# A two-layer encoder in split float32: the neighbourhood bias is loaded with its mask folded in, three weight tiles get their low parts by accumulating transfers, a fourth moves to VectorE, and one mean is issued later

## The chip, the cores and the metric

The program runs on one core of one Trainium2 chip. The metric is the device time of one execution in microseconds; before the change the median of three runs is 1551.98 us (1550.17 to 1553.2). Besides the times there is one execution taken with the hardware profiler. Its engines are called PE (TensorE), DVE (VectorE), ACT (ScalarE), POOL (GpSimd) and SP (SyncE, which here only issues transfers).

## What is computed

Two layers of an encoder on 512 positions of width 1024, all in float32. The parts that the change touches:

```python
mem_n = rms_norm(mem, mem_norm_g)                     # 256 memory tokens
for l in range(DEPTH):                                # 2
    h = rms_norm(x, g_pre_mix[l])
    proj = h @ w_in[l]                                # 1024 -> 5632: q,k,v of A and B, q of M, gates
    o_a = neighborhood_attention(...)                 # 6 heads, s = q.k*scale + bias, softmax, @ v
    o_b = dilated_attention(...)
    o_m = memory_attention(q_m, mem_n, w_mem_kv[l])   # kv = mem_n @ w_mem_kv[l]
    merged = sum of sigmoid gates * (o_x @ w_br_x)
    x = x + rms_norm(merged @ w_out[l], g_post_mix[l])
    h = rms_norm(x, g_pre_ffn[l])
    u = depthwise_conv_centred(h @ w_up[l], conv_w[l], conv_b[l])
    a, b = split(u)
    x = x + rms_norm((gelu(a) * b) @ w_down[l], g_post_ffn[l])
```

In neighbourhood attention each query sees a window of 8 rows by 16 columns of the 8 x 64 grid. The kernel computes 256 candidate keys for each block of 128 queries and adds to the scores a bias by relative position; keys outside the window get -1e30.

## The kernel before, in words

**Split matmuls.** Every float32 operand of a large matmul is held as two tiles in the PE's rounded float32 format (float32r): a high part, which is the rounded value, and a low part, which is the rest. `mm3` (line 249) issues three matmuls for one product: high x high, high x low of the activations, low of the weights x high. So the low part of a weight tile is first read by the third matmul of a trio.

**Weights.** `weights` (line 227) loads a tile of 128 x 1024 numbers (512 KB) on SP's queue into one of three `wraw` buffers, then `split` (line 223) makes the parts: ACT copies `wraw` into the high tile and, by default, DVE subtracts (`tensor_sub`) to make the low tile. With `eng` the subtraction goes to POOL. Tiles that are loaded ahead of their use are split in two halves of 512 columns, each with its own pair of buffers `m` (pool of 32) or `h`.

**Order of the work.** The order on PE is written by the program: `Woven` keeps a modelled PE clock, and jobs (Python generators) are resumed when the clock has reached their due time; `yield 3.5` means "go on 3.5 us of modelled PE time later". PE's instructions are chained in that order. A job that asks for a mean too early makes PE wait for the sums. The order on the other engines comes out of a scheduler that works from the same program; each engine takes its instructions strictly in order.

**The stretch between the layers.** The last product of layer 0 (`sublayer_end`, line 815, with the weights `w_down`) is finished for columns 0 to 255 first, then for 256 to 511. For the first half `end_job` (line 379) takes a mean of squares (a matmul with a column of 1/1024, tile `mean`), spreads it over the partitions by a transpose (matmul with `ident`), multiplies the eight output tiles `y` by it and adds them to `x` on DVE, squares `x` on ACT and adds the squares up on DVE (`acc`). Then `pre_norm_job` (line 364) asks for the next mean from that `acc`. Meanwhile PE works on the memory projection of layer 1 (`mem_kv`, line 479, four tiles of `w_kv`, here called kv0 to kv3) and then, in `run_group` (line 501), on six tiles of `w_in` (g0 to g5). These ten tiles are fetched ahead by `kv_ahead` (line 1013) and line 1029. Which engine makes a tile's low part is read from two strings in line 38: `KVE` for kv0 to kv3 and `GEN` for g0 to g5 (V for DVE, G for POOL). In `KVE` the first letter is unused, since kv0 always takes DVE. For the second half `raw_end_job` (line 418) does the same with tiles `ka` that are not normed yet, and asks for its last mean `yield 3.5` after its squares (line 436).

**The bias.** `a_bias` (line 593) runs one head ahead of `a_head_job`. On POOL's queue it fetches 128 x 256 numbers for a head, and POOL then makes three tiles `mask - bias` (128 x 256, line 599), for the left edge, the middle and the right edge of the grid. The constant `mask` (384 KB) comes in at the start. k is scaled by -0.125, so that PE's scores are negated; DVE adds the negated bias and takes the minimum in one instruction (line 617).

Of the kernel before, what the change touches and what calls it, by code (L numbers as in the profile page):

```python
# [7 lines left out]
F32 = mybir.dt.float32  # L8
# [7 lines left out]
GRID_W = 64  # L16
# [21 lines left out]
SQG, LOG, GEN, KVE = {0: (), 1: ()}, {0: (), 1: ()}, 'GGVGVG', 'VVGG'  # L38
# [81 lines left out]
def tile_hybrid_encoder(ctx, tc, xT, memT, memg, vecs, rpb, w_in, w_kv, w_bra, w_brb, w_brm,  # L120
                        w_out, w_up, w_down, c_ident, c_mask, c_tab0, c_tab1, out):
# [58 lines left out]
    DUP, MDUP = G, G  # L180
    MSQ = G
# [31 lines left out]
    mask = const.tile([128, 3, 256], F32, name="mask")  # L213
# [204 lines left out]
    def raw_end_job(l, goff, og, acc, acc2, nxt, lat):  # L418
# [17 lines left out]
        yield 3.5  # L436
# [156 lines left out]
    def a_bias(l, h):  # L593
        n01, n2r = ytile((128, 2, 256)), ytile((128, 2, 256))
        raw = n2r[:, 1, :]
        behind(nc.gpsimd.dma_start(out=raw, in_=rpb[l, h]).ins, last_lo.get(G))
        neg = (n01[:, 0, :], n01[:, 1, :], n01[:, 1, :], n2r[:, 0, :])
        for c, n in ((0, neg[0]), (1, neg[1]), (2, neg[3])):
            nc.gpsimd.tensor_sub(n, mask[:, c, :], raw)
        return neg  # L600

    def a_head_job(l, h, qkv, neg, oa):
# [293 lines left out]
    for t, c in ((mask, c_mask), (tab0, c_tab0), (tab1, c_tab1)):  # L896
        nc.sync.dma_start(out=t, in_=c)
# [4 lines left out]
    for l in range(depth):  # L902
# [99 lines left out]
        else:  # L1002
# [10 lines left out]
            def kv_ahead(l=l, pre=pre, gw=gw):  # L1013
                pre.append(weights(w_kv[l + 1, 0], KD, 128, htile))
                yield KVD
                for i in (1, 2, 3):
                    yield 0.9
                    pre.append(weights(w_kv[l + 1, i], KD, 128, big, G if KVE[i] == 'G' else V))
                wv.give(f"kv{l + 1}")
                for m in range(NG):  # L1020
                    yield GWD
                    gw.extend(group_weights([w_in[l + 1, FIRST[m]]], [G if GEN[m] == 'G' else V]))
# [6 lines left out]
            gw += group_weights([w_in[l + 1, m] for m in FIRST[NG:]], [G if e == 'G' else V for e in GEN[NG:]])  # L1029
# [4 lines left out]
def _consts():  # L1034
# [4 lines left out]

    mask = np.empty((3, 128, 256), f32)  # L1040
    for n, b in enumerate((0, 1, 3)):
        c = 16 * b + np.arange(16)
        kc = 16 * b - 8 + np.arange(32)
        start = np.clip(c - 8, 0, GRID_W - 16)[:, None]
        ok = (kc[None, :] >= start) & (kc[None, :] < start + 16)
        ok = np.broadcast_to(ok.reshape(1, 16, 2, 1, 16), (8, 16, 2, 8, 16)).reshape(128, 256)
        mask[n] = np.where(ok, 0.0, BIG)
    mask = np.ascontiguousarray(mask.transpose(1, 0, 2))
# [5 lines left out]
    for s in range(2):  # L1054
# [5 lines left out]
    return {"c_ident": ident, "c_mask": mask,  # L1060
            "c_tab0": tab0, "c_tab1": tab1.reshape(128, 2, 256)}


def _layout(inputs):
# [9 lines left out]
    def cols(v):  # L1074
# [13 lines left out]
    a["rpb"] = np.ascontiguousarray(pad[:, :, r - i + 7, 16 * t + c - 8 - cc + 31].reshape(L, NA_HEADS, 128, 256))  # L1088
# [13 lines left out]
        "c_ident", "c_mask", "c_tab0", "c_tab1"]  # L1102
# [22 lines left out]
```

## Time and profile before

| what | us |
|---|---|
| median of 3 runs | 1551.98 |
| the profiled execution, device time | 1551.73 |
| its span, first to last instruction | 1550.0 |
| PE busy | 1522.5 (98%) |
| DVE busy | 951.6 (61%) |
| ACT busy | 712.7 (46%) |
| POOL busy | 149.7 (10%) |

The span begins with the first instruction and ends with the last; all positions below are microseconds in it. "Idle before" of an instruction is the time for which its engine had nothing running, with the engine or transfer that let it go on. The granted clock is the share of TensorE's full speed that the throttle let through. Layer 0 lies up to about 800 us, layer 1 behind.

### The profile page before, as it was taken

The numbers are of one execution on the slowest core, as the hardware profiler recorded it, in microseconds if no ns is written. First come the engines' busy times: TensorE is split into PE (matmuls) and PEld (weight loads), VectorE is DVE, ScalarE is ACT, GpSimd is POOL, SyncE is SP. The second block draws the span as 40 slices with busy tenths as digits, with TensorE's granted clock in tenths as the row PEclk, the third lists the DMA queues.
The fourth block names the chain that finished last, engine by engine and source line by source line (L and its number), as shares of the span: only waits on it lengthen the run. The fifth ranks groups of instructions, "written<-read, shape, count | busy, mean of one in ns | idle before, by whom it ended". The sixth has DMA issues, their size and how long they took to land.

```text
span 1550.0 us, 20648 instructions
## 1 busy us (share of the span) xinstructions
PE 1522.5 (98%) x7970; PEld 1300.1 (84%) x7970; DVE 951.6 (61%) x1684; ACT 712.7 (46%) x1266; POOL 149.7 (10%) x217
## 2 busy tenths in 40 slices
PE   8999999999999999999989999999999999999997
PEld 7988888888988888888888888888889888888887
DVE  6685676335777777742497756753456977776233
ACT  5565554336544444532355555532354544444231
POOL 3340000110000000000154300002100000000000
PEclk9999999999999999999999999999999999999999
DMA  7221213235113322333431221132350233323331
GB/s 246 89 88 64 62 57 107 84 95 165 53 59 100 100 96 95 118 90 101 129 102 59 78 66 58 61 104 88 102 177 15 82 96 99 101 99 89 99 105 63
DMA packets 45810, 144.91 MB, mean 93 GB/s; under 512 B 5376, under 2 KB 9600, under 8 KB 45712
## 3 DMA queue, kind: packets, MB, share of 16 engines
q1 hardware_dynamic: 43776, 139.85, 28.5%
q10 hardware_dynamic: 1296, 2.10, 0.4%
q0 software_dynamic: 640, 1.64, 0.3%
q8 instruction: 62, 1.02, 0.3%
q14 instruction: 36, 0.29, 0.1%
HBM read 141.48 MB, written 2.10 MB: 93 GB/s over the span
## 4 chain that ended last, share of the span: by engine, by line
PE 91%; DVE 6%; ACT 2%; issue 1%; DMA 0%; SPq 0%; ACTq 0%; DVEq 0%
PE mm L247 80%; PE s L247 4%; PE o L247 3%; PE pt L258 2%; DVE m L114 1%; DVE y L114 1%; PE pt L247 1%; DVE ka L114 1%; DVE x L114 1%; ACT y L114 1%; DVE st L114 0%; DVE acc L114 0%; DMA x<-in_xT_dram 0%; DVE wlo L114 0%; ACT whi L114 0%
## 5 line engine op out<-in xcount | busy, mean ns | idle before, releaser
L247 PE MATMUL mm<-h,whi 128*128 128x512 f32 x2496 | 776.5, 392 | 0.0
L247 PEld LDWEIGHTS mm<-h,whi 128*128 128x128 f32 x2496 | 462.0, 188 | 91.3
L247 PE MATMUL mm<-h,wlo 128*128 128x512 f32 x1248 | 486.9, 390 | 0.0
L114 DVE TENSOR_TENSOR wlo<-wraw,whi 128x1024 fp32r<-128x1024 f32 (+1 forms) x213 | 259.2, 1217 | 284.7 <-ACT whi L114 282.3
L114 ACT CAST whi<-wraw 128x1024 fp32r<-128x1024 f32 (+1 forms) x213 | 221.4, 1040 | 307.8 <-PE mm L247 293.4
L247 PEld LDWEIGHTS mm<-h,wlo 128*128 128x128 f32 x1248 | 234.5, 188 | 49.6
L247 PE MATMUL mm<-m,whi 128*128 128x512 f32 (+1 forms) x800 | 215.1, 356 | 1.0 <-DVE m L114 0.8
L247 PEld LDWEIGHTS mm<-m,whi 128*128 128x128 f32 x800 | 141.8, 189 | 22.8 <-PE mm L247 1.3
L247 PE MATMUL mm<-m,wlo 128*128 128x512 f32 (+1 forms) x400 | 142.1, 355 | 0.0
L114 DVE SCALAR_TENSOR_TENSOR y<-y,vec,y 128x511 f32<-128x511 f32 x176 | 130.5, 748 | 3.5 <-ACT y L114 0.9
L114 DVE TENSOR_TENSOR y<-mm,R 128x512 f32<-128x512 f32 x82 | 56.4, 688 | 68.5 <-PE mm L247 68.5
L247 PEld LDWEIGHTS mm<-m,wlo 128*128 128x128 f32 x400 | 75.5, 189 | 10.9
L802 POOL TENSOR_TENSOR m<-m,y 128x512 f32<-128x512 f32 x28 | 36.1, 1289 | 399.4 <-DVE y L114 399.4
L114 ACT ACTIVATE y<-y,vec 128x512 f32<-128x512 f32 x88 | 71.1, 815 | 2.3 <-DVE y L114 1.9
L247 PE MATMUL mm<-m,m 128*128 128x512 f32 x240 | 63.5, 394 | 0.0
L114 ACT ACTIVATE y<-y 128x512 f32<-128x512 f32 x44 | 27.9, 633 | 71.7 <-DVE y L114 71.3
L114 ACT CAST m<-pt 128x512 fp32r<-128x512 f32 (+1 forms) x72 | 38.6, 541 | 46.8 <-PE pt L258 38.5
L114 ACT ACTIVATE y<-y,st 128x256 f32<-128x256 f32 (+1 forms) x80 | 43.8, 549 | 30.4 <-DVE st L114 28.9
L114 DVE TENSOR_TENSOR acc<-acc,sq 128x256 f32<-128x256 f32 (+1 forms) x80 | 41.1, 514 | 26.6 <-ACT sq L114 24.7
L114 DVE TENSOR_TENSOR m<-pt,m 128x512 fp32r<-128x512 f32 (+1 forms) x72 | 45.1, 630 | 19.9 <-ACT m L114 18.6
L114 ACT CAST m<-y 128x512 fp32r<-128x512 f32 x32 | 19.9, 622 | 72.5 <-DVE y L114 72.5
L247 PE MATMUL mm<-h,m 128*128 128x256 f32 x312 | 49.1, 301 | 2.0 <-ACT h L114 1.0
(154 smaller groups left out, 1789.9 us busy)
## 6 DMA issues: line engine op xcount, KB each, us to landing
wraw<-in_w_in_dram SPq DMA_DIRECT2D x88, 512.0 KB, 3.7
wraw<-in_w_up_dram SPq DMA_DIRECT2D x88, 512.0 KB, 3.6
wraw<-in_w_down_dram SPq DMA_DIRECT2D x32, 512.0 KB, 3.5
wraw<-in_w_out_dram SPq DMA_DIRECT2D x16, 512.0 KB, 3.9
wraw<-in_w_down_dram SPq DMA_DIRECT2D x16, 384.0 KB, 3.1
wraw<-in_w_kv_dram SPq DMA_DIRECT2D x8, 512.0 KB, 4.0
wraw<-in_w_bra_dram SPq DMA_DIRECT2D x16, 192.0 KB, 2.3
x<-in_xT_dram SPq DMA_DIRECT2D x8, 256.0 KB, 7.3
```

Source lines behind the costliest of these rows:

```text
L114: return op(*args, **kw)
L247: wv.pe(nc.tensor.matmul(ps, a, b, start=first, stop=last), cost)
L258: wv.pe(nc.tensor.transpose(ps[:, 128 * i:128 * i + 128], s, ident), 0.11)
L802: (V if br == 2 and m >= 6 else G).tensor_add(acc[m], acc[m], gs)
```

## The change

1. The host lays out the bias with the mask in it, three tables for each head instead of one; `a_bias` fetches them with two transfers on POOL's queue (256 and 128 KB) and computes nothing. `mask`, its load and the 36 subtractions on POOL are gone. k is scaled by +0.125, and line 617's instruction adds the bias and scales by -1.
2. In the strings, kv2, kv3 and g0 become `D`, and g1 becomes `V`. For `D`, ACT writes the high part and then, with a second instruction, minus the rounded value into the low tile; a transfer on POOL's queue then reads the weights from HBM again and adds them to the low tile (`accum_op=ALU.add`), for each half tile of 256 KB.
3. `raw_end_job` waits 5.0 instead of 3.5 us of modelled time before its last mean.

```diff
-SQG, LOG, GEN, KVE = {0: (), 1: ()}, {0: (), 1: ()}, 'GGVGVG', 'VVGG'
+SQG, LOG, GEN, KVE = {0: (), 1: ()}, {0: (), 1: ()}, 'DVVGVG', 'VVDD'
...
+    ENG = {'G': G, 'V': V, 'D': 'D'}
...
-    mask = const.tile([128, 3, 256], F32, name="mask")
...
             hi, lo = slot(F32R, (128, c, C)), slot(F32R, (128, c, C))
-            split(raw[:, k:k + c, :], hi, lo, eng)
+            if eng == "D":
+                last_copy[0] = ACT.copy(hi, raw[:, k:k + c, :]).ins
+                ACT.activation(lo, raw[:, k:k + c, :], AF.Copy, scale=-1.0)
+                nc.gpsimd.dma_start(out=lo, in_=src[:, k:k + c, :], accum_op=ALU.add)
+            else:
+                split(raw[:, k:k + c, :], hi, lo, eng)
...
         for k in range(KD):
             sumsq_add(acc2[:, half], xh(k, half), k == 0)
-        yield 3.5
+        yield 5.0
...
-        twice_split(ps, inner[:2], inner[2:], -0.125, DUP)
+        twice_split(ps, inner[:2], inner[2:], 0.125, DUP)
...
     def a_bias(l, h):
-        n01, n2r = ytile((128, 2, 256)), ytile((128, 2, 256))
-        raw = n2r[:, 1, :]
-        behind(nc.gpsimd.dma_start(out=raw, in_=rpb[l, h]).ins, last_lo.get(G))
-        neg = (n01[:, 0, :], n01[:, 1, :], n01[:, 1, :], n2r[:, 0, :])
-        for c, n in ((0, neg[0]), (1, neg[1]), (2, neg[3])):
-            nc.gpsimd.tensor_sub(n, mask[:, c, :], raw)
-        return neg
+        n01, n2r = ytile((128, 2, 256)), ytile((128, 256))
+        nc.gpsimd.dma_start(out=n01, in_=rpb[l, h, :, 0:2, :])
+        nc.gpsimd.dma_start(out=n2r, in_=rpb[l, h, :, 2, :])
+        return n01[:, 0, :], n01[:, 1, :], n01[:, 1, :], n2r
...
-                V.tensor_tensor_reduce(out=S[:, b2, :], in0=s[:, b2, :], in1=neg[b],
-                                               op0=ALU.add, op1=ALU.min, accum_out=m, scale=1.0, scalar=3e38)
+                V.tensor_tensor_reduce(out=S[:, b2, :], in0=s[:, b2, :], in1=pos[b],
+                                               op0=ALU.add, op1=ALU.min, accum_out=m, scale=-1.0, scalar=3e38)
...
-    for t, c in ((mask, c_mask), (tab0, c_tab0), (tab1, c_tab1)):
+    for t, c in ((tab0, c_tab0), (tab1, c_tab1)):
         nc.sync.dma_start(out=t, in_=c)
...
+    a["rpb"] = np.ascontiguousarray(np.where(np.stack(ok, 1), tab, tab.dtype.type(-BIG)))
```

What the change moves is shown by the order of the instructions on two engines. First POOL between the layers, before the change: behind the squares of the memory norm (`h<-h,sq`) stand the low parts (`m`) of kv2, kv3, g0 and g1, two each, and then the copies for `mem_kv`.

```order
L321 TENSOR_TENSOR h_1221_6214<-h_1221_6214,sq_1228_6234 128x256
L225 TENSOR_TENSOR m_6923<-wraw_6920,m_6922 128x512
L225 TENSOR_TENSOR m_6927<-wraw_6920,m_6926 128x512
L225 TENSOR_TENSOR m_6982<-wraw_6979,m_6981 128x512
L225 TENSOR_TENSOR m_6986<-wraw_6979,m_6985 128x512
L225 TENSOR_TENSOR m_7004<-wraw_7001,m_7003 128x512
L225 TENSOR_TENSOR m_7008<-wraw_7001,m_7007 128x512
```

The same place after the change.

```order
L326 TENSOR_TENSOR h_1221_6200<-h_1221_6200,sq_1228_6220 128x256
L245 DMA m_6909<-in_w_kv_dram 128x512
L245 DMA m_6914<-in_w_kv_dram 128x512
L245 DMA m_6970<-in_w_kv_dram 128x512
L245 DMA m_6975<-in_w_kv_dram 128x512
L245 DMA m_6994<-in_w_in_dram 128x512
L245 DMA m_6999<-in_w_in_dram 128x512
L298 COPY m_7063<-m_7063 64x256
```

The subtractions of kv2, kv3 and g0 have become six transfers in the same order, and the two of g1 (before, next behind the rows shown) are gone from POOL.

ACT at the same place, after the change: `m<-wraw` with CAST is a high part, with ACTIVATE the negated one that a transfer adds to; `st` is the root of the mean of the first half, `acc` and `sq` are its squares of `x`.

```order
L114 CAST m_6908<-wraw_6906 128x512
L114 ACTIVATE st_6897<-pt_6894,eps 128x2
L114 ACTIVATE m_6909<-wraw_6906 128x512
L114 CAST m_6913<-wraw_6906 128x512
L114 ACTIVATE m_6914<-wraw_6906 128x512
L114 CAST m_6969<-wraw_6967 128x512
L114 ACTIVATE m_6970<-wraw_6967 128x512
L114 ACTIVATE acc_6067<-x 128x256
L114 ACTIVATE sq_1337_6928<-x 128x256
L114 CAST m_6974<-wraw_6967 128x512
```

Before the change three high parts stood between the root and `acc`; now these are two high parts and three negated ones, and three more negated ones stand further on among the squares.

Next PE at the last mean of `raw_end_job`, before the change: `mm<-ka,m` are products of the raw second half with g0 and g1, three matmuls for each weight tile and each of eight `ka` tiles.

```order
L247 MATMUL mm_7273<-ka_7298,m_7026 128x256
L247 MATMUL pt_7516<-mean,acc_6081 128x1 x2
L247 MATMUL mm_7272<-ka_7299,m_7003 128x256 x2
L247 MATMUL mm_7272<-ka_7299,m_7004 128x256
L247 MATMUL mm_7273<-ka_7299,m_7025 128x256 x2
L247 MATMUL mm_7273<-ka_7299,m_7026 128x256
L247 MATMUL mm_7272<-ka_7300,m_7007 128x256 x2
L247 MATMUL mm_7272<-ka_7300,m_7008 128x256
L247 MATMUL mm_7273<-ka_7300,m_7029 128x256 x2
L247 MATMUL mm_7273<-ka_7300,m_7030 128x256
L247 MATMUL pt_7516<-ident,st_7519 128x128 x2
```

And after the change, from the third `ka` tile on.

```order
L252 MATMUL mm_7265<-ka_7290,m_7018 128x256
L252 MATMUL mm_7264<-ka_7291,m_6993 128x256 x2
L252 MATMUL mm_7264<-ka_7291,m_6994 128x256
L252 MATMUL mm_7265<-ka_7291,m_7017 128x256 x2
L252 MATMUL mm_7265<-ka_7291,m_7018 128x256
L252 MATMUL mm_7264<-ka_7292,m_6998 128x256 x2
L252 MATMUL mm_7264<-ka_7292,m_6999 128x256
L252 MATMUL mm_7265<-ka_7292,m_7021 128x256 x2
L252 MATMUL mm_7265<-ka_7292,m_7022 128x256
L252 MATMUL pt_7520<-mean,acc_6067 128x1 x2
```

The mean stands 12 matmuls later, and its transposes follow, as before, 12 matmuls behind it; nothing else on PE has another place.

More of the change, by code (lines that the diff above doesn't have):

```diff
@@ L120, in tile_hybrid_encoder @@
 def tile_hybrid_encoder(ctx, tc, xT, memT, memg, vecs, rpb, w_in, w_kv, w_bra, w_brb, w_brm,
-                        w_out, w_up, w_down, c_ident, c_mask, c_tab0, c_tab1, out):
+                        w_out, w_up, w_down, c_ident, c_tab0, c_tab1, out):
     nc = tc.nc
@@ L593, in a_bias, with a_head_job @@
     def a_bias(l, h):
-        n01, n2r = ytile((128, 2, 256)), ytile((128, 2, 256))
-        raw = n2r[:, 1, :]
-        behind(nc.gpsimd.dma_start(out=raw, in_=rpb[l, h]).ins, last_lo.get(G))
-        neg = (n01[:, 0, :], n01[:, 1, :], n01[:, 1, :], n2r[:, 0, :])
-        for c, n in ((0, neg[0]), (1, neg[1]), (2, neg[3])):
-            nc.gpsimd.tensor_sub(n, mask[:, c, :], raw)
-        return neg
-    def a_head_job(l, h, qkv, neg, oa):
+        n01, n2r = ytile((128, 2, 256)), ytile((128, 256))
+        nc.gpsimd.dma_start(out=n01, in_=rpb[l, h, :, 0:2, :])
+        nc.gpsimd.dma_start(out=n2r, in_=rpb[l, h, :, 2, :])
+        return n01[:, 0, :], n01[:, 1, :], n01[:, 1, :], n2r
+    def a_head_job(l, h, qkv, pos, oa):
         qs, ks, vs = qkv
@@ L767, in attention_job @@
     def attention_job(l, qkva, qkvb, qm, km, vm, oa, ob, om):
-        neg = a_bias(l, 0)
+        pos = a_bias(l, 0)
         for h in range(NA_HEADS):
@@ L771, in attention_job @@
             nxt = a_bias(l, h + 1) if h + 1 < NA_HEADS else None
-            wv.spawn(a_head_job(l, h, qkva, neg, oa))
-            neg = nxt
+            wv.spawn(a_head_job(l, h, qkva, pos, oa))
+            pos = nxt
             yield STEP_A
@@ L1017, in kv_ahead @@
                     yield 0.9
-                    pre.append(weights(w_kv[l + 1, i], KD, 128, big, G if KVE[i] == 'G' else V))
+                    pre.append(weights(w_kv[l + 1, i], KD, 128, big, ENG[KVE[i]]))
                 wv.give(f"kv{l + 1}")
@@ L1021, in kv_ahead @@
                     yield GWD
-                    gw.extend(group_weights([w_in[l + 1, FIRST[m]]], [G if GEN[m] == 'G' else V]))
+                    gw.extend(group_weights([w_in[l + 1, FIRST[m]]], [ENG[GEN[m]]]))
                 wv.give(f"gw{l + 1}")
@@ L1028, in tile_hybrid_encoder @@
             wv.need(f"gw{l + 1}")
-            gw += group_weights([w_in[l + 1, m] for m in FIRST[NG:]], [G if e == 'G' else V for e in GEN[NG:]])
+            gw += group_weights([w_in[l + 1, m] for m in FIRST[NG:]], [ENG[e] for e in GEN[NG:]])
             wv.need(f"h{l + 1}.{V_PRE}.0")
@@ L1038, in _consts @@
     ident = np.eye(128, dtype=f32)
[L1040 to L1048, printed above, removed]
     slopes = (f32(2.0) ** (-f32(8.0) * np.arange(1, 7, dtype=f32) / f32(6.0))).astype(f32)
@@ L1059, in _consts @@
         tab1[:, s, 1] = np.where(dj % 4 == 0, slopes[4 + s] * d, BIG)
-    return {"c_ident": ident, "c_mask": mask,
-            "c_tab0": tab0, "c_tab1": tab1.reshape(128, 2, 256)}
+    return {"c_ident": ident, "c_tab0": tab0, "c_tab1": tab1.reshape(128, 2, 256)}
 def _layout(inputs):
@@ L1087, in _layout @@
     i, cc, t, r, c = np.ogrid[:8, :16, :2, :8, :16]
-    a["rpb"] = np.ascontiguousarray(pad[:, :, r - i + 7, 16 * t + c - 8 - cc + 31].reshape(L, NA_HEADS, 128, 256))
+    tab = pad[:, :, r - i + 7, 16 * t + c - 8 - cc + 31].reshape(L, NA_HEADS, 128, 1, 256)
+    ok = []
+    for b in (0, 1, 3):
+        q = 16 * b + np.arange(16)
+        key = 16 * b - 8 + np.arange(32)
+        start = np.clip(q - 8, 0, GRID_W - 16)[:, None]
+        inside = (key[None, :] >= start) & (key[None, :] < start + 16)
+        ok.append(np.broadcast_to(inside.reshape(1, 16, 2, 1, 16), (8, 16, 2, 8, 16)).reshape(128, 256))
+    a["rpb"] = np.ascontiguousarray(np.where(np.stack(ok, 1), tab, tab.dtype.type(-BIG)))
     a["w_in"] = tiles(g["w_in"], 128)
@@ L1101 @@
 _INS = ["xT", "memT", "memg", "vecs", "rpb", "w_in", "w_kv", "w_bra", "w_brb", "w_brm", "w_out", "w_up", "w_down",
-        "c_ident", "c_mask", "c_tab0", "c_tab1"]
+        "c_ident", "c_tab0", "c_tab1"]
 def kernel(**inputs):
```

## The prediction

> **What bounds the kernel now.** PE is busy for 98% of the span, so time can only come from what PE does or from the few places where it stands. PE's instructions are the same before and after, but for one pair that moves; so the question is which of PE's waits go and which come. The list of PE's waits comes first (total, times, longest):
>
> ```profile
> PE pt L247 <- DVE acc L114: 4.6, 2, 3.5
> PE pt L247 <- DVE y L114: 3.2, 4, 2.0
> PE pt L258 <- DVE y L114: 2.1, 1, 2.1
> ```
>
> The first line is two waits for sums of squares (`acc`), both between the layers; the third is one wait in a head of layer 1. The second lies in the start, where the sums of the input are made. PE's timeline places the first:
>
> ```profile
> 777.09 3.04 PE L247 MATMUL mm<-h,m 128*128 128x256 f32 x24
> 783.59 0.58 PE L247 MATMUL pt<-mean,acc 128*128 128x1 f32 x4 [3.46 <-DVE acc L114]
> 784.03 1.62 PE L247 MATMUL mm<-h,m 128*128 128x256 f32 x9
> 785.76 0.69 PE L342 MATMUL pt<-ident,st 128*128 128x128 f32 x2
> 786.10 4.79 PE L247 MATMUL mm<-h,m 128*128 128x256 f32 x30
> ```
>
> PE ends kv1 at 780.13 and stands 3.46 us for the mean of `pre_norm_job`. Behind the wait it is slow as well: 24 matmuls took 3.04 us before it (0.127 each), 30 took 4.79 after it (0.160). The stretches with the granted clock (the figure ahead of the last two) say why:
>
> ```profile
> 785.00:787.00 2.00, 1.90 (x10) 1.61 (x9) 1.57 (x6) 0.64 (x3) 1.87 (x6) 0.50 0.04 8
> 787.00:789.00 2.00, 2.00 (x14) 2.00 (x14) 1.85 (x6) 0.80 (x2) 0.26 (x1) 0.69 0.00 0
> 812.00:815.00 3.00, 1.84 (x17) 1.67 (x16) 1.44 (x4) 0.26 (x1) 2.94 (x8) 1.00 0.13 40
> 872.00:875.00 3.00, 1.88 (x7) 1.59 (x8) 1.71 (x3) 1.00 (x2) 2.69 (x5) 0.76 0.00 0
> 875.00:878.00 3.00, 3.00 (x14) 2.47 (x14) 1.52 (x3) 1.70 (x3) 0.56 (x1) 0.67 0.04 4
> ```
>
> After this wait the clock was 0.50 for two microseconds and 0.69 for two: 2 x 0.50 + 2 x 0.31 = 1.6 us of work lost. So this wait costs 3.46 + 1.6 = 5.1 us.
>
> What is it that made `acc` late? DVE's timeline in that stretch:
>
> ```profile
> 767.21 1.29 DVE L114 TENSOR_TENSOR m<-wraw,m 128x512 fp32r<-128x512 f32 x2 [0.45 <-ACT m L114]
> ...
> 769.75 0.75 DVE L114 TENSOR_TENSOR y<-y,pt 128x256 f32<-128x256 f32 x2 [0.93 <-PE pt L342]
> 770.41 2.22 DVE L114 TENSOR_TENSOR x<-x,y 128x256 f32<-128x256 f32 x2
> 772.56 0.74 DVE L114 TENSOR_TENSOR y<-y,pt 128x256 f32<-128x256 f32 x2
> ...
> 783.02 0.76 DVE L114 TENSOR_TENSOR acc<-acc,sq 128x256 f32<-128x256 f32 x2 [0.21 <-ACT sq L114]
> ```
>
> The eight tiles take 8 multiplications, 8 additions to `x` and 7 additions to `acc`, 23 instructions of one size. Started at 0.33 us intervals (two in 0.75 us, the last ending 0.41 after its start), they would take 7.7 us. They took from 769.75 to 783.4, 13.7 us. The multiplications, which read PSUM and SBUF, run at full pace; additions that read two tiles of SBUF are stretched (2.22 us for two). At the same time POOL subtracts low parts:
>
> ```profile
> 768.30 6.93 POOL L225 TENSOR_TENSOR m<-wraw,m 128x512 fp32r<-128x512 f32 x5 [105.56 <-ACT m L114]
> 776.61 4.24 POOL L225 TENSOR_TENSOR m<-wraw,m 128x512 fp32r<-128x512 f32 x3 [1.39 <-ACT m L114]
> ```
>
> POOL's 11.2 us cover most of the stretch; I read the 6 us that DVE loses as the price of sharing a way into SBUF with POOL. These eight subtractions are what the change takes from POOL.
>
> **The change part by part.**
>
> *The wait at 783.59.* POOL no longer subtracts there. DVE gets g1's two low parts, 1.29 us by the row at 767.21: 769.75 + 7.7 + 1.3 = 778.8. ACT gets six negated copies. What it does there now:
>
> ```profile
> 768.51 1.65 ACT L114 CAST m<-wraw 128x512 fp32r<-128x512 f32 x3
> 771.23 0.42 ACT L114 ACTIVATE acc<-x 128x256 f32<-128x256 f32 x1 [1.06 <-DVE x L114]
> ```
>
> A copy is 0.55 us. From 768.51 ACT has 3 + 4 old copies, 6 new ones and 8 squares at 0.33: 13 x 0.55 + 8 x 0.33 = 9.8, so the last square is at 778.3 if ACT never waits, and the sum behind it at 778.7. Either way `acc` is ready before PE comes at 780.13, with 1.3 us to spare. I take the whole 5.1 us; the ends are 0 and 5.1.
>
> *The accumulating transfers.* The trace shows none. They must land before PE reads the low parts. In the new order kv2's first half can be issued after one more copy on ACT (769.1) and POOL's issue (0.56, below), so at 769.6. PE reaches its third matmul at 780.13 + 0.58 + 0.25 = 780.9; kv2's other half 12 matmuls (1.5) later; kv3 24 matmuls (3.05) behind kv2; g0 behind 48 matmuls (6.1) and the two pairs of transposes at about 787.7, and its second half, as g0 and g1 alternate, 24 matmuls on at 790.7. The last issue is behind ACT's copies at about 776.5. So each has 11 us or more. The nearest rows are plain transfers of the same size (KB each, median to landing):
>
> ```profile
> x<-in_xT_dram SPq DMA_DIRECT2D x8, 256.0 KB, 7.3
> wraw<-in_w_brm_dram SPq DMA_DIRECT2D x8, 256.0 KB, 2.7
> ```
>
> The 7.3 is with eight in flight at the start. Landing at either is in time if they overlap. If they went strictly one behind the other, p us each, the sixth would land at 769.6 + 6p, against 790.7: late from p = 3.5 on (the fourth and fifth, by the same working, from 4.05 and 3.6). I take nothing, nearest to 2.7, which is a row of the running kernel and not of its start; the ends are 0 and 6 x 7.3 - 21.1 = 22.7 us of standing, plus 1.6 for the clock.
>
> A rule speaks against these transfers. The Trainium skill (SBUF — State Buffer, the warning on "DVE blocks DMA" under "SBUF: two separate sides") says that POOL's transfers need descriptors written by GpSimd, which cannot be written while DVE runs a two-port instruction. The page's example is 3100 ns in place of 620, so by it each transfer would land some 2.5 us later (an estimate from the page), which 11 us of room take in: the sum would be the same, but the rival below of slow transfers gains by it. No row here shows a starved transfer.
>
> *The later mean.*
>
> ```profile
> 810.20 2.29 PE L247 MATMUL mm<-ka,m 128*128 128x256 f32 x18
> 813.64 0.58 PE L247 MATMUL pt<-mean,acc 128*128 128x1 f32 x4 [1.16 <-DVE acc L114]
> 814.08 1.66 PE L247 MATMUL mm<-ka,m 128*128 128x256 f32 x12
> 815.58 0.38 PE L342 MATMUL pt<-ident,st 128*128 128x128 f32 x2
> ```
>
> PE stands 1.16 us here, and the clock stays at 1.00 (stretch from 812). Behind 12 more matmuls (1.5 us) the mean comes at 814.0, when `acc` was ready at 813.6 even with POOL in the way:
>
> ```profile
> 803.83 0.56 POOL L596 DMA_DIRECT2D y<-in_rpb_dram  x1
> 808.18 2.62 POOL L599 TENSOR_TENSOR y<-mask,y 128x256 f32<-128x256 f32 x3 [3.79 <-DVE ka L114]
> ```
>
> and that subtraction is gone too. Gain 1.16. The mean's followers move by 0.4 us against the start of these matmuls, and PE is 1.16 us earlier; PE next needs the normed half here:
>
> ```profile
> 829.26 0.63 PE L247 MATMUL mm<-h,whi 128*128 128x512 f32 x2
> ```
>
> and DVE has it ready long before:
>
> ```profile
> 821.89 0.75 DVE L114 TENSOR_TENSOR h<-h,h 128x256 fp32r<-128x256 f32 x2
> ```
>
> 829.26 - 1.16 - (822.64 + 0.4) leaves 5 us. So nothing is given back; the ends are 0 and 1.16.
>
> *The bias.* 36 subtractions leave POOL, and 12 more transfers come, 0.56 us of POOL each. Only one wait of PE in the heads is long:
>
> ```profile
> 873.12 0.55 PE L258 MATMUL pt<-ident,y 128*128 128x128 f32 x3 [2.09 <-DVE y L114]
> ```
>
> ```profile
> 871.06 0.35 DVE L114 TENSOR_SCALAR y<-y,st 128x256 f32<-128x256 f32 x1
> ...
> 872.24 0.83 DVE L114 TENSOR_SCALAR y<-y,st 128x256 f32<-128x256 f32 x1
> ```
>
> ```profile
> 871.52 2.13 POOL L599 TENSOR_TENSOR y<-mask,y 128x256 f32<-128x256 f32 x3 [1.07 <-DMA y<-in_rpb_dram]
> ```
>
> The scaling that PE waits for took 0.83 instead of 0.35 us beside POOL's mask subtractions: 0.48 goes. The rest of the wait, 1.6 us, is DVE's order, which stays. Whether the clock then still falls (3 x 0.24 + 3 x 0.33 = 1.7 us from 872 on) is open: 1.6 lies midway between 1.16, where it didn't, and 2.09, where it did. I take 0.5, with the clock falling; the ends are 0 and 2.09 + 1.7 = 3.8.
>
> *The start.* The mask's load goes, and the first two heads' bias is fetched ahead of g3's low parts:
>
> ```profile
> 24.12 2.71 POOL L225 TENSOR_TENSOR m<-wraw,m 128x512 fp32r<-128x512 f32 x2 [9.09 <-ACT m L114]
> ```
>
> Three of the four issues fit in POOL's idle time; one, 0.56 us, stands between the halves. I count nothing, hidden by the matmuls of g3's first half; the ends are -0.4 and 0.6.
>
> *Sum.* 5.1 + 1.16 + 0.48 = 6.7 us. The profiled execution, 1551.73 (span 1550.0 and 1.7 around it), becomes 1545.0. It lies 0.25 below the median of 1551.98; so 1545.3 is forecast.
>
> **The rivals.**
>
> *The clock doesn't fall at 873* (chance 0.15). The Trainium skill (TensorE: Matmul & The Clock Gate, Part 1) puts the fall behind a full idle window of about 3.4 us. By that rule the 2.09 us wait should not have slowed PE, and the trace says it did, at 0.67; the measurement decides, but a 1.6 us wait may well be harmless. Then 1.7 more is won: 1543.6.
>
> *Half the wait stays* (0.12). DVE and ACT wait for each other at each square, which the two chains worked out above leave out. If `acc` comes midway between 778.8 and 785 (the old end and g1's 1.3), PE stands 1.8 us, near the 2.09 that cost clock: 3.46 - 1.8 = 1.7, with the others 3.4, 1548.6.
>
> *POOL is not what slowed DVE* (0.09), so the change doesn't do what its move promises. DVE's 13.7 us plus 1.3 end at 784.7; PE stands 4.6 instead of 3.46. Then -1.1 + 1.16 + 0.5 = 0.5, 1551.5. Against it: the multiplications from PSUM beside POOL are not stretched, the additions are.
>
> *The transfers are slow and in a row* (0.14): slower than before. At p = 4 PE stands 2.9 us and loses 1.6 of clock, 1549.8; the gain is used up at p = 4.4; from 4.9 on it is slower by over 3.1 us; at p = 7.3 it is 22.7 + 1.6 - 6.7 = 17.6 slower, 1569.6. For it: each must read the low tile and write it back, so it moves more than a plain one. Against it: no row shows a transfer that waits for the one ahead to land, and even the 7.3 was reached by eight that flew together. 0.05 for the middle, 0.09 for slower.
>
> **How the numbers follow.** The forecast has 0.50. A difference of 0.2%, 3.1 us (1548.9 to 1555.1), is about the least that a measurement of this kernel can tell from none. Faster: 0.50 + 0.15 + 0.12 = 0.77. Same: 0.09 + 0.05 = 0.14. Slower: 0.09. The range goes from the whole of the wait at 873 won (3.3 more than counted) and 0.4 at the start, 1541.6, to the transfers at p = 4, 1549.8; outside lie 0.09 and 0.09.
>
> **What would show it.** Right: no PE wait of over 1 us for `acc`, DVE's 23 instructions ending before 780, a clock of 1.00 from 780 to 800, the wait at 873 at about 1.6. Wrong: PE waiting for a transfer at `mm<-h,m` of kv2, kv3 or g0; `x<-x,y` still at over 1 us with POOL idle; a new wait behind 829.

## The result and the profile after

The changed kernel takes 1541.01 us (median of 4 runs, 1540.77 to 1542.24); the kernel before took 1551.46 beside it (median of 4, 1550.17 to 1553.2). The ratio is 0.9939, with a 95% interval of 0.9927 to 0.9952: 9.5 us less (7.4 to 11.3). Here and below, a ratio and its interval come from the undisturbed runs of both kernels (one of 5408 us of the kernel before is left out, for example) and are not the quotient of the two medians (0.9933 here). The forecast was 1545.3; the median lies 0.6 us below the lower end of the range, 1541.6. The profiled execution has a span of 1539.3 us against 1550.0.

The list of PE's waits (total, times, longest) has no line for `acc` any more; the head's wait (the third line here, from L258 before) is 1.3 and not 2.1.

```profile
PE pt L252 <- DVE y L114: 2.6, 3, 1.5
PE pt L263 <- ACT sq L114: 1.7, 2, 0.9
...
PE pt L263 <- DVE y L114: 1.3, 1, 1.3
```

PE's timeline at kv1's end, where 3.46 us of waiting stood, and at the second half's mean, where 1.16 stood:

```profile
776.14 3.04 PE L252 MATMUL mm<-h,m 128*128 128x256 f32 x24
779.02 0.50 PE L252 MATMUL pt<-mean,acc 128*128 128x1 f32 x4
779.38 1.31 PE L252 MATMUL mm<-h,m 128*128 128x256 f32 x9
780.54 0.38 PE L347 MATMUL pt<-ident,st 128*128 128x128 f32 x2
780.67 3.85 PE L252 MATMUL mm<-h,m 128*128 128x256 f32 x30
...
804.15 3.71 PE L252 MATMUL mm<-ka,m 128*128 128x256 f32 x30
807.70 0.50 PE L252 MATMUL pt<-mean,acc 128*128 128x1 f32 x4
```

Neither mean has an "idle before", and 30 matmuls behind the first take 3.85 us instead of 4.79. The stretches behind it, with the granted clock as the third figure from the end, are at 1.00 where before they were at 0.50 and 0.69:

```profile
785.00:787.00 2.00, 2.00 (x19) 2.00 (x19) 1.80 (x6) 1.60 (x6) 0.00 (x0) 1.00 0.08 10
787.00:789.00 2.00, 2.00 (x20) 2.00 (x19) 1.91 (x5) 1.52 (x5) 0.00 (x0) 1.00 0.02 4
```

DVE's timeline ahead of the mean:

```profile
768.79 0.75 DVE L114 TENSOR_TENSOR y<-y,pt 128x256 f32<-128x256 f32 x2 [0.93 <-PE pt L347]
769.47 0.75 DVE L114 TENSOR_TENSOR x<-x,y 128x256 f32<-128x256 f32 x2
...
776.22 0.69 DVE L114 TENSOR_TENSOR m<-wraw,m 128x512 fp32r<-128x512 f32 x1 [0.33 <-ACT m L114]
...
777.16 0.69 DVE L114 TENSOR_TENSOR m<-wraw,m 128x512 fp32r<-128x512 f32 x1
777.76 0.75 DVE L114 TENSOR_TENSOR acc<-acc,sq 128x256 f32<-128x256 f32 x2
```

Two additions to `x` take 0.75 us (2.22 before). Of the two additions to `acc` in the last row only the first belongs to this mean; the other adds up squares of the second half's products (`sq<-mm`), as the second one at 783.02 did before. So the last sum ends at 778.2, 9.4 us behind the first multiplication, with g1's subtractions among them (13.7 without them before). PE comes at 779.0, so there are 0.8 us to spare, where 1.3 were forecast.

The accumulating transfers (KB each, median from issue to landing) take longer than the 2.7 that the prediction leant on, and longer than its far end of 7.3 too. PE waits for none of them. The first line is a plain transfer of the same size on the same queue: the new bias, spread over the whole kernel.

```profile
y<-in_rpb_dram POOLq DMA_DIRECT2D x12, 256.0 KB, 3.5
...
m<-in_w_kv_dram POOLq DMA_DIRECT2D x4, 256.0 KB, 7.8
...
m<-in_w_in_dram POOLq DMA_DIRECT2D x2, 256.0 KB, 10.7
```

In layer 1's head, PE's timeline and then DVE's: the scalings are at full pace, and the wait is 1.26 instead of 2.09.

```profile
864.58 0.55 PE L263 MATMUL pt<-ident,y 128*128 128x128 f32 x3 [1.26 <-DVE y L114]
```

```profile
860.00 0.60 DVE L114 TENSOR_SCALAR y<-y,st 128x256 f32<-128x256 f32 x2
...
864.16 0.36 DVE L114 TENSOR_SCALAR y<-y,st 128x256 f32<-128x256 f32 x1
```

The clock stays at 1.00 here too:

```profile
864.00:867.00 3.00, 2.42 (x14) 2.10 (x15) 1.43 (x4) 1.83 (x3) 0.45 (x2) 1.00 0.11 37
```

**Where the span went.** PE does the same work in both kernels, so its instructions can be used as milestones. The first column of the table is a position, that of PE's stand for `sq` near 77 us (layer 0); the others give the time between milestones, from PE's timelines: from that stand to the first half's mean, on to its stand for `sq` near 839, on to the wait in the head, and on to the span's end. The lines of the experiments are used further down.

| kernel | stand at 77 | to the mean | to 839 | to the head | to the end |
|---|---|---|---|---|---|
| before | 77.23 | 706.36 | 55.99 | 33.54 | 676.8 |
| after | 76.28 | 702.74 | 53.10 | 32.46 | 674.8 |
| transfers only | 75.13 | 702.71 | 54.62 | 33.05 | 675.2 |
| mean only | 77.16 | 706.29 | 54.47 | 33.44 | 675.3 |
| bias only | 75.87 | 706.34 | 54.70 | 32.48 | 674.8 |
| after, mean back | 77.02 | 702.71 | 53.16 | 32.47 | 674.8 |
| after, all on VectorE | 76.53 | 702.71 | 54.92 | 32.48 | 674.9 |
| before, POOL's part left out | 75.46 | 702.69 | 54.19 | 33.50 | 675.3 |
| after, eight transfers | 76.50 | 702.71 | 54.42 | 32.46 | 674.8 |
| after, ten transfers | 77.35 | 702.73 | 57.60 | 32.52 | 674.9 |
| before, second profile | 77.83 | 706.23 | 56.13 | 33.00 | 675.4 |
| before, third profile | 78.65 | 706.29 | 56.70 | 33.14 | 675.4 |

In the pair of profiles the change wins 0.95 in the start, 3.62 to the mean, 2.89 behind it, 1.08 ahead of the head and 2.06 from there on: 10.6 us, where the prediction's sum was 6.7. The theory that went into the experiments: the first mean is worth 5 us and due to POOL alone; the later mean is worth about 1; the bias is worth more than the 0.48 counted, because the clock no longer falls in the head; the start is chance.

### The profile page after: what moved, and what is told of

It reads as the page before. It is cut to its first block, busy times and chain, and to the rows that moved or that the text cites. A ratio compares the mean times of both kernels' runs of the same rounds, so it can differ in the third digit from the quotient of the medians.

```text
span 1539.3 us, 20627 instructions
## 1 busy us (share of the span) xinstructions
PE 1518.5 (99%) x7970; PEld 1297.4 (84%) x7970; DVE 941.2 (61%) x1686; ACT 713.2 (46%) x1272; POOL 122.9 (8%) x191
## 4 chain that ended last, share of the span: by engine, by line
PE 94%; DVE 3%; ACT 1%; issue 1%; DMA 0%; SPq 0%; ACTq 0%
PE mm L252 82%; PE s L252 5%; PE o L252 4%; PE pt L263 2%; PE pt L252 1%; DVE m L114 1%; DVE y L114 1%; DVE ka L114 0%; DMA x<-in_xT_dram 0%; ACT y L114 0%; DVE wlo L114 0%; DVE h L114 0%; DVE st L114 0%; ACT whi L114 0%; PE pt L347 0%
## 5 line engine op out<-in xcount | busy, mean ns | idle before, releaser
L114 DVE TENSOR_TENSOR m<-wraw,m 128x512 fp32r<-128x512 f32 (+1 forms) x60 | 38.4, 653 | 22.8 <-ACT m L114 22.7
```

Of the source, the lines that this page charges most:

```text
L114: return op(*args, **kw)
```

## The experiments

**The transfers alone.**

```diff
 (the kernel before)
-... GEN, KVE = ..., 'GGVGVG', 'VVGG'
+... GEN, KVE = ..., 'DVVGVG', 'VVDD'
 (and the branch eng == "D" of weights)
```

> The kernel before with the three weight tiles' low parts by accumulating transfers and one on VectorE; the bias is still masked by POOL and the mean stands where it stood. My theory, from the two traces: the wait at 783.59 goes (3.46 us) and the slow clock behind it (1.6 to 1.7 us): 5.1 us, so 1546.4 us beside a before of 1551.5; no PE wait for acc at kv1's end; two of DVE's x<-x,y take 0.75 us there and not 2.22; the second mean still waits about 1.2 us, since POOL's mask subtractions still stand beside its sums; the wait in layer 1's head stays at about 2.1 us. Rival 1, the bias was needed for this wait too (POOL comes earlier to the mask subtractions): PE still waits 1 us or more there, 1548 to 1551. Rival 2, the gain at the start (about 0.9 us) comes from this part: first mean matmuls at 8.4 us and not at 10.1, 1545.5 us.

Measured: 1544.54 us beside 1550.64, ratio 0.9967 (0.9955 to 0.9980), 5.1 us less. PE's timeline at the three places, and DVE's additions:

```profile
777.84 0.58 PE L253 MATMUL pt<-mean,acc 128*128 128x1 f32 x4
...
806.53 0.58 PE L253 MATMUL pt<-mean,acc 128*128 128x1 f32 x4 [1.12 <-DVE acc L114]
...
865.51 0.55 PE L264 MATMUL pt<-ident,y 128*128 128x128 f32 x3 [1.59 <-DVE y L114]
```

```profile
768.27 0.75 DVE L114 TENSOR_TENSOR x<-x,y 128x256 f32<-128x256 f32 x2
```

The first wait is gone without the bias (rival 1 falls), the second is still there. By the table, 706.36 becomes 702.71 and 55.99 becomes 54.62: 3.65 us up to the mean, most of it the wait of 3.46, and 1.37 behind it, where the slow clock was; 5.0 us. Not expected: the head's wait is 1.59 and not 2.1, and the clock stays up behind it; more on that below. The start came earlier than in either kernel (first transposes at 9.39 us), which is the sign of rival 2; but this edit does not touch the start, and in kernels without any of these transfers it also came early, at 9.98 with POOL's part left out and at 10.17 with the later mean alone. So rival 2 isn't borne out.

**The later mean alone.**

```diff
 (the kernel before, raw_end_job)
-        yield 3.5
+        yield 5.0
```

> The kernel before with the second half's mean 12 matmuls later, and nothing else. My theory: the wait of 1.16 us at 813.64 goes and nothing is given back at 829, 1.2 us faster: 1550.3 us beside 1551.5. The rival, that PE waits as long elsewhere (the normed half comes 0.4 us later, or the head behind it waits for DVE): 1551.5 us, with a new wait of 0.8 us or more between 815 and 840. As this kernel's start is that of the kernel before, it also tells whether the first mean matmuls at 10.1 us are a fixed property of that start (my theory: yes, within 0.3 us) or vary from run to run by 1 us or more (rival).

Measured: 1548.65 us beside 1550.64, ratio 0.9991 (0.9983 to 1.0000), so 1.4 us less, with an interval that reaches to none.

```profile
813.49 0.51 PE L247 MATMUL pt<-mean,acc 128*128 128x1 f32 x4
...
871.36 0.55 PE L258 MATMUL pt<-ident,y 128*128 128x128 f32 x3 [1.97 <-DVE y L114]
```

No wait at the mean, and by the table 55.99 becomes 54.47: 1.5 us, of which nothing comes back up to the head. This profile's head waits 1.97 us, and the clock did not fall there. The start was not fixed within 0.3 us, as the theory had it: the first transposes came at 10.17 and not at 11.68.

**The bias alone.**

```diff
 (the changed kernel)
-... GEN, KVE = ..., 'DVVGVG', 'VVDD'
+... GEN, KVE = ..., 'GGVGVG', 'VVGG'
-        yield 5.0
+        yield 3.5
```

> The kernel before with the bias loaded with its padding, and nothing else. My theory, from the two traces: layer 1's head waits 1.26 us and not 2.09, and the clock there stays at 1.00: 2.5 us; the start is 0.9 us earlier, with the first mean matmuls at about 8.4 us; the second half's mean, with no mask subtractions beside its sums, waits 0.2 us or less though it stands where it stood: 1.0 us; the wait at 783.59 stays at 3.5 us. Sum 4.4, so 1547.1 us beside 1551.5. The prediction's terms (0.48 in the head with the clock still falling, nothing at the start or at the mean): 1551.0 us. The rival on the start, that it is chance: first mean matmuls at about 10.1 us and 1548.0 us.

Measured: 1547.05 us beside 1550.64, ratio 0.9981 (0.9972 to 0.9990), 2.9 us less.

```profile
782.21 0.58 PE L252 MATMUL pt<-mean,acc 128*128 128x1 f32 x4 [3.47 <-DVE acc L114]
...
811.04 0.50 PE L252 MATMUL pt<-mean,acc 128*128 128x1 f32 x4
...
869.39 0.55 PE L263 MATMUL pt<-ident,y 128*128 128x128 f32 x3 [1.27 <-DVE y L114]
```

The first wait stays whole. The second is gone with the mean in its old place: by the table 1.3 us. The rows show what held `acc` up there: before, beside POOL's subtractions at 808.18, two additions to `acc` and an instruction that makes a `ka` took 0.85 to 0.96 us; here they take 0.42 to 0.48. The head waits 1.27. Against the first profile of before, 33.54 becomes 32.48 and 676.8 becomes 674.8, as the theory had it, but the times show 2.9 (1.6 to 4.3) and not 4.4: the start is not 1.7 us earlier (first transposes at 9.99, among starts of 9.39 to 11.68), and not every run of before has the slow clock in the head.

**The mean back in the changed kernel.**

```diff
 (the changed kernel, raw_end_job)
-        yield 5.0
+        yield 3.5
```

> The changed kernel with the second half's mean back in its old place. The prediction's term: 1.16 us of waiting come back, 1542.2 us beside 1541.0. My theory now: in the changed kernel acc is ready at about 806.0 us and PE would come to the mean at 806.2, so 0 to 0.3 us come back: 1541.0 to 1541.3 us; the removed mask subtractions already do what the later place does.

Measured: 1540.77 us, ratio to before 0.9946 (0.9932 to 0.9960), against the changed kernel's 0.9939: no difference. The table says the same, 53.16 against 53.10.

```profile
807.02 0.50 PE L252 MATMUL pt<-mean,acc 128*128 128x1 f32 x4
```

No wait comes back. So the later mean and the bias are two cures for one wait: alone, each is worth 1.3 to 1.5 us, and behind the bias the later mean is worth nothing. The prediction's separate term for it was right for the sum and wrong for its cause.

**POOL's subtractions left out.**

```diff
 (the kernel before; kv2, kv3, g0 and g1)
-            split(raw[:, k:k + c, :], hi, lo, eng)
+            last_copy[0] = ACT.copy(hi, raw[:, k:k + c, :]).ins
+            lo = hi
```

> The kernel before, in which POOL's eight low-part subtractions between the layers (kv2, kv3, g0, g1) are left out, and PE reads the high part in the low part's place; nothing takes over their work on any engine, bias and mean are as before. If POOL's subtractions are what stretched DVE's additions: two x<-x,y take 0.75 us and not 2.22, DVE's 23 instructions take 7.7 to 9 us and not 13.7, no wait of PE at kv1's end, and 5.0 us less: 1545.6 us beside 1550.6. If something else did (ACT's copies, the weight loads that land in that stretch): 2.2 us for two as before, a wait of 3 us or more, 1550.6 us.

Measured: 1543.06 us beside 1550.88, ratio 0.9952 (0.9939 to 0.9964), 7.4 us less (5.6 to 9.5). DVE, then PE:

```profile
768.59 0.75 DVE L114 TENSOR_TENSOR x<-x,y 128x256 f32<-128x256 f32 x2
```

```profile
778.15 0.50 PE L252 MATMUL pt<-mean,acc 128*128 128x1 f32 x4
...
865.84 0.55 PE L263 MATMUL pt<-ident,y 128*128 128x128 f32 x3 [2.09 <-DVE y L114]
```

With nothing changed but POOL's eight instructions (PE reads the high parts in the low parts' place), DVE's additions are at full pace, PE doesn't wait for the mean, and the time to it is 702.69. So POOL's subtractions, and not the weight loads or ACT's copies, stretched DVE and made PE wait. The Trainium skill (SBUF — State Buffer, "Who interferes with whom") says that a DVE instruction with two SBUF inputs contends with a GpSimd instruction that reads SBUF, through a shared read interface; the rows agree: 2.22 us for two `x<-x,y` beside POOL, 0.75 without, while `y<-y,pt`, with one input in PSUM, stayed at 0.75 in both. The saving in time is larger than the 5.0 expected; the profile has 5.5 of it between 77 and 839 us (3.67 and 1.80 by the table); behind the head it has 1.6 more, since the clock did not fall there, and its start is 1.8 us earlier, which is chance. The last runs show both.

**All low parts on VectorE.**

```diff
 (the changed kernel)
-... GEN, KVE = ..., 'DVVGVG', 'VVDD'
+... GEN, KVE = ..., 'VVVGVG', 'VVVV'
```

> The changed kernel, with the low parts of kv2, kv3 and g0 subtracted on VectorE instead of added by transfers: no accumulating transfer is left, DVE has six more subtractions of 0.6 us, ACT six copies fewer. Theory 1, taking POOL out of this stretch is what won the time, and the transfers are only one way of doing it: kv2's two come ahead of the multiplications, which then start 0.7 us later, and acc is ready at about 779.1 us beside PE's 779.0, so PE waits 0.1 to 0.6 us for it: 1541.1 to 1541.6 us. Theory 2, DVE is too full in this stretch for it (3.9 us more in the chain): PE waits 3 us for acc and the clock falls behind it, 1545 to 1546 us.

Measured: 1543.38 us, ratio to before 0.9949 (0.9935 to 0.9963). There is no wait for `acc` (702.71 to the mean, as in the changed kernel): theory 1 expected 0.1 to 0.6 us of it, and theory 2, with 3 us, falls. But two new waits stand behind:

```profile
790.64 0.40 PE L347 MATMUL pt<-ident,st 128*128 128x128 f32 x2 [0.89 <-DVE st L114]
800.74 5.62 PE L252 MATMUL s<-h,m 128*128 128x256 f32 x45 [0.71 <-DVE m L114]
```

By the table 53.10 becomes 54.92. So the transfers are not what removes the 5 us, since VectorE does it as well. Over VectorE they are worth 1.8 us in this stretch of the profiles, most of it the two new waits for DVE; the times alone can't tell the two apart, as the interval overlaps the changed kernel's (0.9927 to 0.9952). Theory 1's number left these waits out.

**Plain transfers.**

```diff
 (the changed kernel)
-                nc.gpsimd.dma_start(out=lo, in_=src[:, k:k + c, :], accum_op=ALU.add)
+                nc.gpsimd.dma_start(out=lo, in_=src[:, k:k + c, :].bitcast(F32R))
```

> The changed kernel with the six transfers copying the weights into the low tile instead of adding them to the negated copy there (so the low parts are wrong, the instructions and bytes the same but for the adding). If adding is what makes them long: 3 to 5 us from issue to landing instead of 7.8 (kv2, kv3) and 10.7 (g0). If it is the weight loads that share the DMA engines in that stretch: 7 us or more again. The time is that of the changed kernel, 1541 us, within 1 us either way, since no transfer is waited for in either.

Measured: 1540.65 us, one run. The two lines of the transfers:

```profile
m<-in_w_kv_dram POOLq DMA_DIRECT2D x4, 256.0 KB, 5.9
m<-in_w_in_dram POOLq DMA_DIRECT2D x2, 256.0 KB, 5.5
```

Between the two expectations. Adding is what makes 7.8 and 10.7 us out of 5.9 and 5.5. The rest isn't explained by one thing: the 2.7 was a row of SP's queue, and on POOL's queue the bias's plain transfers of the same size take 3.5 elsewhere in the kernel; the other 2.0 to 2.4 us belong to this stretch. Whether the weight loads make them, the six transfers among themselves, or VectorE holding up POOL's queue, as the prediction feared, no run here tells apart. The issue on POOL is dearer too: 0.53 to 0.55 us plain, 0.86 to 0.93 adding. The time is the same, since nothing waits for them.

**Ten transfers, and eight.**

```diff
 (the changed kernel, ten; eight has 'DDVGVG', 'VVDD')
-... GEN, KVE = ..., 'DVVGVG', 'VVDD'
+... GEN, KVE = ..., 'DDVGVG', 'VDDD'
```

> The changed kernel with kv1's and g1's low parts by accumulating transfers too: ten instead of six. In the changed kernel six of 256 KB ran through one another from 769.5 to 784 us, 2.4 us each. At that rate ten take 24 us, from about 766.5 to 791, and g1's second half is read at about 791: at the edge. ACT has four more copies (2.2 us), which puts its last square at about 779.4 and acc at 779.9, beside PE's 779.0. Theory: PE waits 0.5 to 1.5 us for acc and 0 to 2 us for a transfer, 1541.5 to 1545 us. Rival, transfers go side by side whatever their number (landing 8 to 11 us behind the issue as with six): no PE wait for a transfer, 1541 to 1542.5 us. Rival, each more in flight slows all (landing at 15 us or more): PE waits 3 us or more at kv1 or kv2, over 1546 us.

Measured with ten: 1545.60 us, ratio to before 0.9965 (0.9953 to 0.9978).

```profile
781.43 1.34 PE L252 MATMUL mm<-h,m 128*128 128x256 f32 x9 [0.85 <-ACT y L114]
...
790.60 2.21 PE L252 MATMUL mm<-h,m 128*128 128x256 f32 x13 [2.11 <-DMA m<-in_w_in_dram]
```

One wait behind the mean (for ACT, not for `acc` itself) and one for a transfer, just over the theory's 2 us; the time is 0.6 over its upper end. The theory left out that the clock falls behind the second wait, to half for 3.41 us from 791.77 on: between the mean and 839 it is 4.5 us more than the changed kernel, of which the two waits are 3.0.

> The changed kernel with g1's low parts by accumulating transfers too: eight instead of six (with ten, PE stood 2.1 us for one at 790.6 us). With ten, the queue moved 0.43 to 0.53 MB in each 4 us, 2.2 us for 256 KB. At that rate eight that begin at 768.5 us are through at 786 to 787.5, and g1's parts are read from about 787 on: theory, no wait of over 0.3 us for a transfer, and as VectorE's 1.3 us less wins nothing where PE doesn't wait, 1541.0 us, within 0.7. Rival, the price lies in ACT's negated copies and not in the transfers: PE waits 0.5 us or more for acc or for ACT at 779 to 781 us, 1541.7 us or more, and none for a transfer. Rival, the limit is below eight: PE waits 1 us or more for a transfer, 1542 us or more.

Measured with eight: 1542.82 us beside 1549.37, ratio 0.9962 (0.9948 to 0.9975).

```profile
787.60 1.82 PE L252 MATMUL mm<-h,m 128*128 128x256 f32 x13 [0.99 <-DMA m<-in_w_in_dram]
```

The theory falls and the third rival holds, by a hair (0.99 us where it said 1 or more): with eight, PE already stands for a transfer, and the stretch to 839 is 1.3 us longer. The times point the same way, though the intervals of eight and six overlap a little. The changed kernel's six are near the most that this stretch bears. What sets the limit stays open. The bytes of POOL's transfers went through at an even rate at first (0.49, 0.45 and 0.40 MB in the three stretches of 4 us from 772 on with six transfers; 0.45, 0.46, 0.46 and 0.65 in four with eight), which looks like a queue that is always full, or like one that shares with the weight loads: in the last of the four, SP's loads had fallen from 0.71 to 0.17 MB. But the transfer that PE stood for can also be explained by its own latency: g1's first, issued at 777.71 behind ACT's copies, landed at 787.6 after 9.8 us, no longer than the 10.3 that is the median for its kind there.

**The kernel before, twice more.**

> The kernel before, once more, unchanged. For the start: the first transposes of the start at 11.7 us in the first profile; with the same code they stood at 9.4 to 11.7 in others, so theory: anywhere in that band; the rival, that the start of this kernel is fixed: 11.5 to 11.9. For the clock behind the wait in layer 1's head: that wait is 2.0 to 2.1 us again; theory, PE's idle time is counted in windows of 3.41 us that run on their own, and the clock falls only if some 2 us of the wait lie in one of them: a fall in about half of the profiles, so 1550.0 us of span with one and 1548.3 without, but for the start; the rival, a wait of 2.09 us always costs clock: a fall again.

> The same as the run ahead of it, a third profile of the kernel before: theory, a fall of the clock behind the head's wait if, and only if, about 2 us of it lie in one window of 3.41 us, whose edges can be read from the fall behind the mean's wait at 783; the start anywhere between 9.4 and 11.7 us. The rivals: a fall in any case; a start at 11.5 to 11.9 us in any case.

Measured: spans of 1548.6 and 1550.1 us. For the start, the first transposes, in the first, second and third profile of this kernel:

```profile
11.68 0.69 PE L342 MATMUL pt<-ident,st 128*128 128x128 f32 x2 [0.56 <-DVE st L114]
```

```profile
10.81 0.69 PE L342 MATMUL pt<-ident,st 128*128 128x128 f32 x2 [0.55 <-DVE st L114]
```

```profile
11.63 0.69 PE L342 MATMUL pt<-ident,st 128*128 128x128 f32 x2 [0.55 <-DVE st L114]
```

In the profile with the transfers alone, whose start is the same code, they stood at 9.39. So the start varies by up to 2 us of itself, with the landing of the first tiles of `x` (256 KB each, a median of 6.1 us in that profile and of 7.3, 6.6 and 7.6 in the three of before), and the 0.95 us won there in the pair of profiles (10.77 against 11.68) is within that. For the stand at 77 us, six profiles with the old bias give 75.1 to 78.7, seven with the new one 75.8 to 77.4.

The head's wait is not a constant 2.09 either, which neither theory had; it is 1.60 in both. This is the second profile:

```profile
873.19 0.55 PE L258 MATMUL pt<-ident,y 128*128 128x128 f32 x3 [1.60 <-DVE y L114]
```

And the clock stayed at 1.00 behind it in both. To see why, the stretches are cut in steps of 3.41 us, so that an edge falls on the instant at which the records show the rate changing; within a profile all its changes lie whole steps apart (figures: length, PE busy and count, then the other engines, and the clock third from the end). The first profile of before, around both falls:

```profile
781.42:784.83 3.41, 1.24 (x10) 1.27 (x11) 2.64 (x9) 2.31 (x8) 0.79 (x2) 1.00 0.49 154
784.83:788.24 3.41, 3.31 (x17) 3.02 (x16) 2.98 (x9) 1.61 (x5) 2.29 (x6) 0.50 0.02 5
...
870.17:873.58 3.41, 1.32 (x9) 0.89 (x8) 2.77 (x8) 0.60 (x2) 2.34 (x4) 1.00 0.05 17
873.58:876.99 3.41, 3.41 (x12) 2.73 (x12) 1.92 (x2) 2.12 (x3) 1.38 (x4) 0.50 0.00 0
```

The second profile of before, at the first half's mean:

```profile
778.91:782.32 3.41, 1.71 (x15) 1.50 (x13) 3.41 (x7) 0.62 (x2) 2.42 (x2) 1.00 0.49 154
782.32:785.73 3.41, 1.67 (x13) 1.58 (x13) 2.62 (x8) 2.32 (x8) 1.21 (x4) 1.00 0.47 154
785.73:789.15 3.42, 3.02 (x15) 2.93 (x15) 3.02 (x9) 1.17 (x4) 1.86 (x5) 0.50 0.02 5
```

The kernel with POOL's part left out, at the head, where 2.09 us of waiting lie across an edge:

```profile
861.99:865.40 3.41, 1.76 (x9) 1.16 (x7) 3.25 (x9) 1.04 (x4) 2.21 (x4) 1.00 0.20 65
865.40:868.81 3.41, 2.97 (x17) 2.53 (x18) 1.87 (x3) 2.39 (x4) 2.57 (x5) 1.00 0.00 0
```

The same wait of 2.09 us cost clock in one run (1.32 us busy in its window) and none in the other (1.76). In the second profile of before, PE was busy for 1.71 us in one window, and the clock stayed; then for 1.67, and it fell. Over all thirteen profiles, between 770 and 880 us, the clock fell behind each of the seven windows with 1.74 us or more of waiting and began no fall behind any with 1.70 or less. So in this stretch the point looks like half a window, and not the 2 us that the expectation named. That it is half of the window isn't shown. The 1.74 us window holds a mean, whose one-column matmuls the profile counts as busy; of the windows without one, the clock fell behind those with 1.96 us or more and not behind those with 1.70 or less. And at the program's start and end the clock also fell behind windows with less waiting, which held such means too: behind 1.19 us in the third profile of before (PE busy for 2.23 us from 22.29 on, 1.05 of it in eight one-column matmuls) and behind 1.14 us at the end of the later mean alone. Perhaps those hardly count as work there; no run tells. The Trainium skill (TensorE: Matmul & The Clock Gate, Part 1) describes a window of some 3.4 us that runs free of the program, and a fall after an idle window; the runs agree on the length and on the free running, and show that the window need not be idle as a whole.

## Why the prediction held, and where it didn't

**The wait at 783.59: right, in mechanism and size.** 5.1 us were forecast; the transfers alone won 5.0 in the profile and 5.1 in the times, and leaving out POOL's subtractions shows that they were the cause. Both rivals to it fell (half the wait stays; POOL isn't what slowed DVE). The margin was thinner than worked out, 0.8 us and not 1.3: the chain from the first multiplication took 9.4 us instead of 9.0, since DVE does wait for ACT at times (0.33 us at 776.22), which the working left out.

**The transfers: nothing lost, as forecast, but nearer to it than the argument had it.** The step that leant on a plain 2.7 us row was wrong in size: 7.8 and 10.7 us. That row was of SP's queue, and even a plain transfer on POOL's took 5.5 to 5.9 in this place. The 11 us of room covered it. The rival of slow transfers had the right place; with two more of them it comes true, at 0.99 us.

**The later mean: right sum, wrong cause.** The working noted that the mask's subtraction beside these sums goes too, and did not follow it: with it gone, PE would not have waited there in any case. The wait is won once, by either edit.

**The bias in the head: the step that failed.** The prediction took 0.48 us "with the clock falling". The wait became 1.26 and not 1.6: besides the last scaling, the pair of scalings ahead of it is at full pace too (0.60 us at 860.00; 0.99 in the first profile of before, 0.98 in the second), and what stands behind on DVE moves up with it. Why the pair got faster isn't shown: POOL runs two casts beside it in both kernels, and no mask subtraction. The clock did not fall at 1.26, and would not have at 1.6, as the profiles with 1.59, 1.60 and 1.97 us show; this is the first rival. In the pair of profiles the term came to 1.08 + 1.6 us, the latter the clock's (between the head's wait and the next one that both kernels have, 65.11 us became 63.48). Against the other profiles of before, which had no fall to lose, it came to 0.5 to 0.7. So 1.6 us of the pair's 10.6 belongs to one run of before, not to that kernel.

**The start: nothing, as forecast.** The 0.95 in the pair is chance.

**Not in the prediction.** From the start of the last instruction on DVE to the end of the span it takes 3.9 to 4.1 us with the new bias and 4.4 with the old one, in every profile: about 0.4 us. Which part of the edit does it wasn't tried.

**The account.** Predicted 6.7, in the pair 10.6: 0.95 for the start, 0.25 for the two means together, 0.6 for the head's wait, 1.6 for its clock and 0.4 for the end make the 3.9 between them. Of these, the start and the clock are what one run of before happened to pay. The three parts' ratios, taken alone, add up to 5.1 + 1.4 + 2.9 = 9.4 us, against 9.5 for the whole, though one wait is in two of them; the intervals, some 1 to 2 us to each side, are wider than that. That the median lies 4.3 us below the forecast, and even below the range, is in part luck: the forecast starts from 1551.98, and in the later comparisons the kernel before had medians of 1549.4 to 1550.9.

No version that does all the work beats the changed kernel beyond the spread of its runs. Undoing the later mean costs nothing; two or four transfers more, or none, cost 1.3 us or more between the mean and 839.

## What to carry to other kernels

When a chain on VectorE is late, look at what GpSimd reads at that moment before you shorten the chain: eight subtractions on an engine that was 10% busy cost 5 us on the critical one. When two edits touch the same wait, its gain counts once; follow each edit alone through the place. And price a wait of PE of about 2 us not by its length alone but as a wait that in some runs brings 1.6 us of clock with it, as it falls on the clock's windows: compare several profiles of the kernel before, since one of them may have paid that and another not.

## What the hardware showed

- The clock's window: 3.41 us long, running on its own; between the layers and in layer 1's head, 1.74 us of waiting in one brought half rate for the next, 1.70 did not (with the reserve made above). After a wait of 3.44 us across two windows (1.96 and 1.48 us) the rate stayed at half for two, as the third profile of before shows:

```profile
780.05:783.46 3.41, 1.45 (x13) 1.24 (x11) 3.41 (x7) 0.75 (x2) 2.16 (x2) 1.00 0.60 168
783.46:786.87 3.41, 1.93 (x9) 1.96 (x10) 2.62 (x8) 2.19 (x7) 1.47 (x4) 0.50 0.37 139
786.87:790.29 3.42, 3.42 (x18) 3.42 (x18) 2.38 (x8) 1.16 (x3) 1.62 (x5) 0.50 0.02 5
```

- An accumulating transfer of 256 KB into SBUF landed 7.8 to 10.7 us behind its issue (medians) where a plain one at the same place took 5.5 to 5.9, and its issue held POOL for 0.86 us instead of 0.53.
- A scaling on DVE beside POOL's subtractions (`TENSOR_SCALAR`, 128x256) took 0.83 us in some profiles and 0.35 in others of the same kernel, so the head's wait moved between 1.6 and 2.1 us from run to run. It goes with the instant: a scaling that began 0.02 or 0.03 us behind the start of one of POOL's subtractions (some 0.72 us each) took 0.83 to 0.84, one that began 0.16 behind it 0.72, and those that began 0.53 to 0.58 behind it 0.35. The first of the three subtractions begins when the bias has landed, which differs from run to run.
